# Hybrid mLSTM / RWKV-7 / S5 decoder step: the first RWKV column tile's elementwise part is issued ahead of the mLSTM gates and the S5 setup

## The chip, the cores and the metric

One core of one Trainium2 chip runs the whole step. Its engines work side by side, each through its own queue in order: TensorE (PE, with its weight loads as PEld), VectorE (DVE), ScalarE (ACT), GpSimd (POOL), and SyncE (SP), which issues most DMAs. The metric is the device time of one execution in microseconds, the median of the runs shown.

## What is computed

One layer (DEPTH is 1) over 512 prompt rows and 8 sample rows, 520 rows in all, of 1024 columns. A wide projection of the input is cut into the inputs of three mixers, whose outputs are merged and normalised:

```python
def _layer(x, st, p):
    ...
    xm, ig, fg, og, zm, rcols, zr, u, zs, gm = _split_cols(x @ p['w_in'])
    ...                                            # mLSTM branch: gates ig, fg, conv, q, k, v
    xr = rcols + p['r_mu'] * (prev - rcols)        # RWKV-7 branch
    r, kr, vr, wd, ad = jnp.split(xr, [...], axis=-1)
    wlog = -jax.nn.softplus(-_f32(p['r_w0'] + jnp.tanh(wd) @ p['r_w2'])) - 0.5
    decay = jnp.exp(-jnp.exp(wlog))
    a = jax.nn.sigmoid(_f32(p['r_a0'] + ad @ p['r_a2']))
    kk = heads(_f32(kr * p['r_k_k']))
    kk = kk / jnp.maximum(jnp.sqrt(jnp.sum(kk * kk, -1, keepdims=True)), 1e-12)
    ...
    yr, wkv_new = _rwkv7_recurrence(rh, heads(decay), kh, vh, kk, heads(a), _f32(wkv0))
    yr = _head_norm(yr, RWKV_GN_EPS).reshape(bsz, t, R_WIDTH) * _f32(p['r_ln_g']) + _f32(p['r_ln_b'])
    ...
    s_re, s_im = _s5_scan(uf, sre0, sim0, ...)     # S5 branch: lb_im = mag * jnp.sin(lam_im * dt), ...
    ...
    return layer_norm(ALPHA * x + merged @ p['w_out'], p['ln_g'], p['ln_b']), new_state
```

## The kernel before

Rows are kept transposed: a tile is 128 columns by 520 rows (two halves, 256 and 264). Every projection is exact to float32 by three passes: the weight is split into a high part `whi` (copied by ACT, L130) and a low part `wlo` (subtracted on POOL or DVE, L131), and each half is 24 matmuls of 0.12 us in one PSUM tile `g`, of which there are three. So a projected tile is 48 matmuls, about 5.7 us of PE. Whoever empties `g` lets PE go on: ACT for a mixer's own column (`rc` L350, `xr` L351), DVE for tiles projected ahead to fill PE (`us` L278 to L282, `zf` L298). `rcol` projects one RWKV column and may take a queued fill tile first.

The order of the program is: entry LayerNorm (to about 40 us), RWKV (to about 750 us), S5, mLSTM, and the final merge. In `rwkv()` the low-rank inputs come first (`rcol(24)`, Tanh), then the first part of `s5_setup` (it ends with two Sin activations, L834 and L835), then the mLSTM `gates`, then the rest of the S5 setup. Only then come the eight column tiles, in four pairs. For a tile `ct`:

- `decay(ct)`: Exp on both halves of both low-rank products (`ew`, `ta`, L460), Ln (L463), Exp (L464), a cumulative sum `cs` on DVE (L466), and four Exp of it (`pd` L471, `pc` L473, `ip` L476, and of the sample rows `smp` L477).
- `elementwise(ct)`: squares, `ss` by matmul, Relu (L492), then Ln (L494) and Exp (L495) give the reciprocal norm `inv`; DVE makes `kkn` (L497), `ar`, `bk`, `bv`. It calls `decay(ct + 1)` near its end. Last it multiplies `bk` by `pc` and transposes it to `bkt` (L570, L572).
- per pair: `inverse`, a chain of 31 steps of two DVE instructions each (`itmp` L589, `xi` L591), begun by the transpose `lu` (L579); `chain`, matmuls over the chunks with small copies between; `headnorm`, with Ln on two halves (L681) and one Exp (L682) on ACT for each tile.

A scheduler lays out the queues: the order of writing is the priority, and by its own clock it puts an instruction where its operands seem ready. So `decay`, `elementwise` and `headnorm` of the next and the last tiles are strewn through `inverse` and `chain`, and code written elsewhere moves instructions on all engines. At run time each queue goes in that order.

ACT holds one set of function tables at a time; a change of set is an instruction of its own, `ACT_TABLE_LOAD`, which the compiler puts ahead of an activation whose function the loaded set lacks. One of them is written by hand: `A.preload_act_table_set("natural_log_exp_and_others")`, L434, held behind the Tanh and the Sin by `issue_after`.

Of the kernel before, what the change touches and what calls it, by code (L numbers as in the profile page):

```python
# [8 lines left out]
F32 = mybir.dt.float32  # L9
# [6 lines left out]
P = 128  # L16
# [7 lines left out]
RH, RD, CH = 16, 64, 64  # L24
NCH = T // CH
# [14 lines left out]
def hybrid_step(ctx: ExitStack, tc: tile.TileContext, I, O):  # L40
# [317 lines left out]

    env = dict(locals())
    rwkv(tc, I, O, env)  # L360
    flc.close()
    mrg = Merge(tc, I, O, env)
# [29 lines left out]
def rwkv(tc, I, O, env):  # L392
# [3 lines left out]
    dma, pa, pc, mm, tr, pcol, inproj, gemm = e.dma, e.pa, e.pc, e.mm, e.tr, e.pcol, e.inproj, e.gemm  # L396
# [16 lines left out]
    ctx2 = ExitStack()  # L413
    rp = ctx2.enter_context(tc.tile_pool(name="rp", bufs=1, reuse_waits="tile"))
# [3 lines left out]
    def rt(name, tag="t", bufs=TB):  # L418
        return rp.tile([P, N], F32, tag=tag, bufs=bufs, name=name)
# [8 lines left out]
    xwa = rcol(24)  # L428
    th = A.activation(lora[0:64, :], xwa[0:64, :], AF.Tanh)
    V.tensor_copy(lora[64:128, :], xwa[64:128, :])  # L430
    setup = s5_setup(tc, I, O, env)
    sin = next(setup)
    with tc.issue_after(th.ins), tc.issue_after(sin.ins):
        A.preload_act_table_set("natural_log_exp_and_others")  # L434
    gates(tc, I, O, env)
    next(setup, None)
    rq = ctx2.enter_context(tc.tile_pool(name="rq", bufs=1, reuse_waits="tile"))

    def halves(f):
        for s, n in HALVES:  # L440
            f(s, n)
# [8 lines left out]
    def decay(ct):  # L450
        for j, nm in enumerate(("r_w2", "r_a2")):
            dma(w2a2[hs(j), j], I[nm][0, :, ct * P:(ct + 1) * P])

        ew, ta = rt("ew"), rt("ta")

        def lo1(s, n):
            for j, (t, b) in enumerate(((ew, e.nw0), (ta, e.na0))):
                p = pa("lw")
                mm(p[:, 0:n], w2a2[:, j], lora[:, s:s + n])
                A.activation(t[:, s:s + n], p[:, 0:n], AF.Exp, bias=b[:, ct:ct + 1], scale=-1.0)  # L460
        halves(lo1)
        for t in (ew, ta):
            A.activation(t, t, AF.Ln, bias=epst[:, 4:5])  # L463
            A.activation(t, t, AF.Exp, scale=-1.0)  # L464
        cs = rt("cs")
        V.tensor_tensor_scan(cs[:, 0:T], cstep.rearrange("p a b -> p (a b)"), ew[:, 0:T], 0.0,  # L466
                             op0=ALU.mult, op1=ALU.add)
        pd = rp.tile([P, NCH, CH + 1], F32, tag="pd", bufs=1, name="pd")
        G.memset(pd[:, :, 0:1], 1.0)
        cs3 = f3(cs)  # L470
        A.activation(pd[:, :, 1:CH + 1], cs3, AF.Exp, scale=-EH)  # L471
        pcs = rp.tile([P, NCH], F32, tag="pc", bufs=4, name="pc")
        A.activation(pcs, cs3[:, :, CH - 1], AF.Exp, scale=-EH)  # L473
        ip = rt("ip")
        ip3 = f3(ip)
        A.activation(ip3, cs3, AF.Exp, scale=EH)  # L476
        A.activation(smp[:, ct, 0, :], ew[:, T:N], AF.Exp, scale=-EH)  # L477
        return ta, pd, ip3, pcs

    def elementwise(ct, st):  # L480
        ci = ct % 2
# [16 lines left out]
        ar = rp.tile([P, 2, NCH, 2 * CH], F32, tag="ar", bufs=4, name="ar")  # L498
# [3 lines left out]
        bk = rp.tile([P, NCH, 3 * CH], F32, tag="bk", bufs=1, name="bk")  # L502
# [21 lines left out]
        bv = rt("bv", "bv", 3)  # L524
# [8 lines left out]
        yv = st["yv"]  # L533
# [8 lines left out]
        la, lr = st["la"], st["lr"]  # L542
# [17 lines left out]
                                pattern=[[0, 4], [1, 2], [1, 64]], channel_multiplier=-1)  # L560
        if ct < KT - 1:
            decays.append(decay(ct + 1))
        G.tensor_tensor(bk, bk, st["pc"][ci].unsqueeze(2).to_broadcast([P, NCH, 3 * CH]), op=ALU.mult)
        bkt = rq.tile([P, 2, NCH, CH], F32, tag="bkt", bufs=4, name="bkt")
        pvs = [pa("bt").rearrange("p (a b) -> p a b", a=NCH) for _ in range(2)]
# [103 lines left out]
    def headnorm(ct, y, bv, w):  # L669

        rng = ((0, 256), (256, 256)) if w == T else ((0, w),)
        q = rq.tile([P, T], F32, tag="yq", bufs=1, name="yq")
        for s, n in rng:
            p = pc("hm")
            mm(p[:, 0:n], e.cen, y[:, s:s + n])
            A.activation(y[:, s:s + n], p[:, 0:n], AF.Copy)
            A.activation(q[:, s:s + n], p[:, 0:n], AF.Square)
        for s, n in rng:
            p = pc("hv")
            mm(p[:, 0:n], e.bones, q[:, s:s + n])  # L680
            A.activation(q[:, s:s + n], p[:, 0:n], AF.Ln, scale=1.0 / RD, bias=epst[:, 2:3])  # L681
        A.activation(q[:, 0:w], q[:, 0:w], AF.Exp, scale=-0.5)  # L682
        V.scalar_tensor_tensor(y, y, pcol("r_ln_g", ct), q[:, 0:w], op0=ALU.mult, op1=ALU.mult)
        V.tensor_tensor(bv[:, 0:w], y, bv[:, 0:w], op=ALU.add)

    decays = [decay(0)]
    for s_ in range(4):
        st = {"ar": [0, 0], "bkt": [0, 0], "bv": [0, 0]}
        st["pc"] = [0, 0]
        st["yv"] = rp.tile([P, 2, 2, NCH, RD], F32, tag="yv", bufs=2, name="yv")  # L690
        st["la"] = rp.tile([P, 2 * NCH, CH], F32, tag="la", bufs=1, name="la")
        st["lr"] = rp.tile([P, 2 * NCH, CH], F32, tag="lr", bufs=2, name="lr")
        for ci in range(2):
            elementwise(2 * s_ + ci, st)
        inverse(st)
        yr = chain((2 * s_, 2 * s_ + 1), st)
        for ci in range(2):
            ct = 2 * s_ + ci
            bv = st["bv"][ci]
            headnorm(ct, yr[:, ci, :], bv, T)  # L700
            dma(e.ybsave[ct, :, 0:T], bv[:, 0:T])
# [19 lines left out]
    for c4 in range(2):  # L721
        p = pa("s48")
        for j in range(4):
            ct = 4 * c4 + j
# [978 lines left out]
```

## Time and profile before

| | |
|---|---|
| time, median of 3 runs | 1435.56 us (1435.4 to 1437.0) |
| the profiled execution's own time | 1430.04 us |
| its span, first to last instruction | 1428.2 us |
| mean granted TensorE clock | 0.954 |
| PE busy | 1291.1 us, 90% |
| DVE busy | 952.2 us, 67% |
| ACT busy | 618.3 us, 43% |
| POOL busy | 568.4 us, 40% |

The span is 1.8 us shorter than the same execution's time: what lies outside the first and the last instruction. In the rows further below, a stretch of a window is read by its length and each engine's busy time in it: an engine busy for the whole stretch is its limit. A timeline row gives the start, the length, and in brackets the idle time before an instruction and what ended it.

### The profile page before, as it was taken

What the parts mean: (1) busy time and instruction counts of PE and PEld (TensorE: products, weight loads), DVE (VectorE), ACT (ScalarE), POOL (GpSimd) and SP (SyncE); (2) the same over time, 40 slices, a digit from 0 to 9 for tenths busy, and PEclk for the clock granted to TensorE, in tenths of its full rate; (3) what the DMA queues carried; (4) which work ended last, traced back from release to release, by engine and by line L of the source; (5) the groups of instructions that cost most, each with busy time, mean ns of one, the idle gap of its engine ahead of it and who ended that gap; (6) DMA issues with size and microseconds to landing.
All of it is one profiled execution on the core that took longest, in us unless ns stands there. A gap on an engine that the chain in (4) does not pass through costs nothing.

```text
span 1428.2 us, 27605 instructions
## 1 busy us (share of the span) xinstructions
PE 1291.1 (90%) x10509; PEld 1162.1 (81%) x10509; DVE 952.2 (67%) x1950; ACT 618.3 (43%) x1322; POOL 568.4 (40%) x723
## 2 busy tenths in 40 slices
PE   5889989998999899998996888897899999999897
PEld 4888888877987788997976788787888798799765
DVE  6784693469336843789535997577775784665857
ACT  4446537354735463241232332232765775443230
POOL 3445544444444454447406775872000012103710
PEclk9999999999998999998998899997899999999999
DMA  5342222212221222344427453434767676466241
GB/s 181 84 117 81 80 74 63 75 42 68 66 71 42 79 64 75 96 129 149 122 69 131 105 104 91 102 77 117 225 198 255 212 224 207 149 197 194 82 118 60
DMA packets 244275, 166.92 MB, mean 117 GB/s; under 512 B 54424, under 2 KB 219674, under 8 KB 243870
## 3 DMA queue, kind: packets, MB, share of 16 engines
q1 hardware_dynamic: 244142, 165.15, 41.3%
q8 instruction: 83, 1.36, 0.4%
q14 instruction: 50, 0.41, 0.1%
HBM read 124.13 MB, written 38.68 MB: 114 GB/s over the span
## 4 chain that ended last, share of the span: by engine, by line
PE 52%; DVE 22%; POOL 8%; DMA 8%; issue 6%; ACT 3%; SPq 1%; DVEq 0%; ACTq 0%; POOLq 0%
PE g L62 33%; PE cy L62 3%; DVE xi L591 3%; DVE itmp L589 3%; PE cr L62 2%; PE gg L62 2%; POOL ph L954 1%; DVE wlo L131 1%; POOL pht L952 1%; POOL pht L953 1%; PE qk L62 1%; PE nd L62 1%; POOL et L981 1%; PE s L62 1%; PE lw L62 1%
## 5 line engine op out<-in xcount | busy, mean ns | idle before, releaser
L62 PE MATMUL g<-xh,whi 128*128 128x264 f32 (+1 forms) x1552 | 463.3, 299 | 40.2 <-DVE th L1500 15.0
L62 PE MATMUL g<-xl,whi 128*128 128x264 f32 (+1 forms) x1552 | 458.0, 295 | 1.0 <-POOL xl L217 0.5
L62 PE MATMUL g<-xh,wlo 128*128 128x264 f32 (+1 forms) x1552 | 457.2, 295 | 0.0
L62 PEld LDWEIGHTS g<-xh,whi 128*128 128x128 f32 x1552 | 303.6, 196 | 52.3 <-DVE th L1500 16.4
L62 PEld LDWEIGHTS g<-xl,whi 128*128 128x128 f32 x1552 | 303.9, 196 | 6.2 <-POOL xl L217 0.8
L62 PEld LDWEIGHTS g<-xh,wlo 128*128 128x128 f32 x1552 | 303.5, 196 | 4.9 <-issue 0.8
L130 ACT ACTIVATE whi<-wraw 128x512 fp32r<-128x512 f32 x258 | 151.6, 625 | 222.0 <-PE g L62 152.1
L131 POOL TENSOR_TENSOR wlo<-wraw,whi 128x512 fp32r<-128x512 f32 x138 | 192.7, 1416 | 134.7 <-ACT whi L130 122.6
L131 DVE TENSOR_TENSOR wlo<-wraw,whi 128x512 fp32r<-128x512 f32 x120 | 111.6, 956 | 29.5 <-ACT whi L130 27.4
L591 DVE TENSOR_TENSOR xi<-xi,itmp 128x31 f32<-128x31 f32 (+15 forms) x124 | 56.6, 456 | 3.2
L589 DVE TENSOR_TENSOR itmp<-lu,xi 128x31 f32<-128x31 f32 (+15 forms) x124 | 53.9, 435 | 3.0
L555 DVE TENSOR_TENSOR lr<-gg,maskg 64x256 f32<-64x256 f32 x32 | 13.5, 422 | 59.9 <-ACT la L554 59.8
L650 DVE SCALAR_TENSOR_TENSOR xv<-xv,pc,cy 64x64 f32<-64x64 f32 x112 | 31.2, 279 | 29.5 <-PE cy L62 24.9
L637 POOL COPY xv<-yv 64x128 f32<-64x128 f32 x64 | 24.8, 389 | 58.6 <-PE cy L62 48.2
L1547 POOL TENSOR_TENSOR mg<-mg,gth 128x256 f32<-128x256 f32 (+1 forms) x24 | 18.4, 782 | 72.6 <-DVE gth L1546 59.5
L62 PE MATMUL g<-ysh,whi 128*128 128x256 f32 (+1 forms) x128 | 38.3, 311 | 7.9 <-ACT ysh L258 5.6
L62 PE MATMUL g<-w_bmh,wlo 128*128 128x264 f32 (+1 forms) x128 | 37.5, 294 | 7.5 <-DVE wlo L131 7.4
L1547 POOL TENSOR_TENSOR mg<-mg,gt 128x256 f32<-128x256 f32 (+1 forms) x16 | 16.1, 1011 | 67.3 <-DVE gt L1546 67.3
L298 DVE COPY zf<-g 128x256 f32<-128x256 f32 (+1 forms) x56 | 23.8, 424 | 28.7 <-PE g L62 28.3
L644 DVE COPY yv<-cr 64x128 f32<-64x128 f32 x32 | 9.0, 281 | 50.2 <-PE cr L62 43.8
L1279 POOL COPY cvo<-xm 128x11 f32<-128x11 f32 x8 | 4.6, 572 | 91.9 <-ACT xm L1277 70.8
L645 ACT COPY yv<-cr 64x128 f32<-64x128 f32 x32 | 8.4, 262 | 75.6 <-DVE yv L644 75.4
(574 smaller groups left out, 3257.2 us busy)
## 6 DMA issues: line engine op xcount, KB each, us to landing
wraw<-in_w_in_dram SPq DMA_DIRECT2D x194, 256.0 KB
zsave<-zf SPq DMA_DIRECT2D x36, 260.0 KB
cn<-in_state_mlstm_c_dram SPq DMA_DIRECT2D x32, 256.0 KB
out_dram<-cn SPq DMA_DIRECT2D x32, 256.0 KB
yb<-yssave SPq DMA_DIRECT2D x16, 260.0 KB
zz<-zsave SPq DMA_DIRECT2D x16, 260.0 KB
wraw<-in_w_br_dram SPq DMA_DIRECT2D x16, 256.0 KB
wraw<-in_s_glu_w_dram SPq DMA_DIRECT2D x16, 256.0 KB
```

The costliest lines, as they stand in the source:

```text
L62: TE.matmul(out, lhsT, rhs, start=start, stop=stop)
L130: A.activation(hi[:, k, 0:m], raw[:, :, 0:m], AF.Copy)
L131: eng.tensor_tensor(lo[:, k, 0:m], raw[:, :, 0:m], hi[:, k, 0:m].bitcast(F32), op=ALU.subtract)
L298: V.tensor_copy(z[:, s:s + n], p)
L589: V.tensor_tensor(tv, lu[:, s + 1:32, s:s + 1].to_broadcast([P, r, w]), xi[:, s:s + 1, 0:w].to_broadcast([P, r, w]), op=ALU.mult)
L591: V.tensor_tensor(xi[:, s + 1:32, 0:w], xi[:, s + 1:32, 0:w], tv, op=ALU.add)
L637: G.tensor_copy(xv[hs(1 - pi), pi], yv[hs(1 - pi), pi, :, n, :])
L650: V.scalar_tensor_tensor(dst, xv[hs(pi), pi, ci, :], pcs[ci][hs(pi), n:n + 1], psn[hs(pi), ci, :], op0=ALU.mult, op1=ALU.add)
L952: G.tensor_tensor(tg[0], b(0), ph[:, q, :, 0:n], op=ALU.mult)
L953: G.tensor_tensor(tg[1], b(1), ph[:, 1 - q, :, 0:n], op=ALU.mult)
L954: G.tensor_tensor(ph[:, q, :, n:2 * n], tg[0], tg[1], op=ALU.add if q else ALU.subtract)
L1547: G.tensor_tensor(dst, dst, g, op=ALU.add)
```

## The change

`elementwise(0)` (with `decay(0)` and `decay(1)`) is written right after the Tanh and the table preload, ahead of `s5_setup` and `gates`. Its last part, the product with `pc` and the transposed rows `bkt`, becomes a function `beta_rows`, called for tile 0 behind the setup and for the others right behind their `elementwise`, as before. The preload loses its hold on the Sin, which is now written behind it.

```diff
     th = A.activation(lora[0:64, :], xwa[0:64, :], AF.Tanh)
     V.tensor_copy(lora[64:128, :], xwa[64:128, :])
-    setup = s5_setup(tc, I, O, env)
-    sin = next(setup)
-    with tc.issue_after(th.ins), tc.issue_after(sin.ins):
+    with tc.issue_after(th.ins):
         A.preload_act_table_set("natural_log_exp_and_others")
-    gates(tc, I, O, env)
-    next(setup, None)
-    rq = ctx2.enter_context(tc.tile_pool(name="rq", bufs=1, reuse_waits="tile"))
...
         if ct < KT - 1:
             decays.append(decay(ct + 1))
+        return ar, bk, bv
+
+    def beta_rows(ct, st, made):
+        ci = ct % 2
+        ar, bk, bv = made
         G.tensor_tensor(bk, bk, st["pc"][ci].unsqueeze(2).to_broadcast([P, NCH, 3 * CH]), op=ALU.mult)
...
     decays = [decay(0)]
+    st = state()
+    made = elementwise(0, st)
+
+    setup = s5_setup(tc, I, O, env)
+    next(setup)
+    gates(tc, I, O, env)
+    next(setup, None)
+    rq = ctx2.enter_context(tc.tile_pool(name="rq", bufs=1, reuse_waits="tile"))
     for s_ in range(4):
-        st = {"ar": [0, 0], "bkt": [0, 0], "bv": [0, 0]}
...
+        if s_:
+            st = state()
         for ci in range(2):
-            elementwise(2 * s_ + ci, st)
+            ct = 2 * s_ + ci
+            beta_rows(ct, st, elementwise(ct, st) if ct else made)
         inverse(st)
```

Line numbers in the pieces of order below are those of the kernel they come from: Sin is L834 in the one, L846 in the other; the Exp, Ln and Exp of `decay` are L460, L463, L464 in the one and L455, L458, L459 in the other; Ln and Exp of `inv` L494, L495 and L489, L490.

ACT's queue around the Tanh (`lora`) and the two Sin (`s`, `c`), before (`gv` are the gates' inputs):

```order
L429 ACTIVATE lora<-xr 64x520
L1131 ACTIVATE gv<-g,gbias 4x256
L834 ACT_TABLE_LOAD
L834 ACTIVATE s<-rr 128x64
L835 ACTIVATE c<-ab,epst 128x64
L434 ACT_TABLE_LOAD
L1131 ACTIVATE gv<-g,gbias 4x264
```

and with the change, first at the Tanh:

```order
L130 ACTIVATE whi<-wraw 128x512
L429 ACTIVATE lora<-xr 64x520
L432 ACT_TABLE_LOAD
L455 ACTIVATE ew<-lw,nw_319 128x256
L455 ACTIVATE ta<-lw,na_321 128x256
```

and some 70 rows on, at the Sin:

```order
L350 ACTIVATE rc<-g 128x264
L351 ACTIVATE xr<-g,omu 128x264
L846 ACT_TABLE_LOAD
L846 ACTIVATE s<-rr 128x64
L847 ACTIVATE c<-ab,epst 128x64
L480 ACTIVATE sq<-xr,par 128x520
```

The preload stood behind the Sin; it now stands ahead of it, with tile 0's Exp and Ln between, and what follows the Sin starts from the set that the Sin's load brought.

ACT's queue in the first `inverse`, where `decay(2)` lies; before:

```order
L460 ACTIVATE ew<-lw,nw_319 128x264
L463 ACTIVATE ew<-ew,epst 128x520
L460 ACTIVATE ta<-lw,na_321 128x264
L464 ACTIVATE ew<-ew 128x520
L130 ACTIVATE whi<-wraw 128x512 x2
L350 ACTIVATE rc<-g 128x264
L463 ACTIVATE ta<-ta,epst 128x520
L572 ACTIVATE bkt<-bt 128x512
L477 ACTIVATE smp<-ew 128x8
```

and with the change:

```order
L455 ACTIVATE ew<-lw,nw_319 128x264
L458 ACT_TABLE_LOAD
L458 ACTIVATE ew<-ew,epst 128x520
L455 ACT_TABLE_LOAD
L455 ACTIVATE ta<-lw,na_321 128x264
L459 ACTIVATE ew<-ew 128x520
L130 ACTIVATE whi<-wraw 128x512 x2
L350 ACTIVATE rc<-g 128x264
L458 ACT_TABLE_LOAD
L458 ACTIVATE ta<-ta,epst 128x520
L572 ACTIVATE bkt<-bt 128x512
L472 ACT_TABLE_LOAD
```

The activations are the same; a load now stands wherever a Ln follows an Exp or an Exp a Ln. It is so at every such place behind the Sin up to the end of the RWKV stage, in `inv` and in `headnorm` too. In all, ACT's queue has 18 loads before and 71 with the change: 54 new ones, less the one at L1499 (the first Tanh of the S5 merge), which is gone. By stage they stand so:

| stage | new loads |
|---|---|
| tile 1's `inv`, ahead of the first `inverse` | 2 |
| first `inverse`: `decay(2)` 4, `inv` 2 | 6 |
| first `chain`: `decay(3)` 2, `inv` 2 | 4 |
| second and third `inverse`: `decay` and `inv` 4, `headnorm` 6, each | 20 |
| second and third `chain`: `decay` 4, `inv` 2, each | 12 |
| fourth `inverse`: `headnorm` of the third pair | 4 |
| fourth `chain` and the end: sample rows 2, last `headnorm` 4 | 6 |

DVE's queue where the last rows of the S5 setup (`pks`, `ph`, `s_`) meet a tile's `kkn`; before, tile 0's:

```order
L892 COPY pks<-c_775 64x32 x2
L875 TENSOR_TENSOR pks<-pw_746,pw_747 128x256
L875 TENSOR_TENSOR s_776<-ph 128x64
L892 COPY pks<-s_776 64x32 x2
L278 COPY us<-g 128x32x8
L497 SCALAR_TENSOR_TENSOR kkn<-xr,par,inv 128x520
```

and with the change, tile 1's:

```order
L887 TENSOR_TENSOR pks<-pw_1321,pw_1322 128x256
L887 TENSOR_TENSOR s_1351<-ph 128x64
L278 COPY us<-g 128x32x8
L904 COPY pks<-s_1351 64x32 x2
L278 COPY us<-g 128x32x8
L281 COPY us<-g 128x8
L282 COPY us<-g 128x8
L492 SCALAR_TENSOR_TENSOR kkn<-xr,par,inv 128x520
```

Gates and setup stood ahead of tile 0's `kkn`; they now stand between tile 0's `bv` and tile 1's `kkn`, and six first copies `us` (L278) lie among them where five did.

## Rows read from the trace of the kernel before

**Rows 1.** The page's busy times: busy us, share of the span, instructions.
```profile
PE 1291.1 (90%) x10509; PEld 1162.1 (81%) x10509; DVE 952.2 (67%) x1950; ACT 618.3 (43%) x1322; POOL 568.4 (40%) x723
```

**Rows 2.** Stretches of the span: length, busy us (instructions) of each engine, granted clock, DMA.
```profile
60.00:80.00 20.00, 13.26 (x78) 11.96 (x77) 15.49 (x64) 5.72 (x12) 5.05 (x6) 0.74 0.42 88
...
163.00:215.00 52.00, 45.24 (x336) 43.10 (x335) 48.51 (x90) 22.78 (x48) 23.11 (x27) 0.93 0.24 66
...
300.00:356.00 56.00, 46.52 (x348) 40.55 (x344) 52.06 (x108) 26.60 (x61) 23.17 (x34) 0.94 0.20 56
356.00:440.00 84.00, 84.00 (x851) 75.18 (x849) 32.09 (x71) 43.73 (x103) 38.00 (x52) 1.00 0.25 68
```

**Rows 3.** ACT's table loads by line: count, busy us, mean ns of one, idle before.
```profile
L1258 ACT ACT_TABLE_LOAD x5 | 6.4, 1283 | 0.1
...
L434 ACT ACT_TABLE_LOAD x1 | 1.3, 1283 | 0.0
```

**Rows 4.** ACT's timeline at a load of the mLSTM stage: start us, us, instruction, [idle before].
```profile
826.38 1.28 ACT L1072 ACT_TABLE_LOAD   x1
828.73 0.41 ACT L1072 ACTIVATE yo<-ys 128x288 f32<-128x288 f32 x1 [1.07 <-PE ys L62]
```

**Rows 5.** ACT's timeline in the first `inverse`.
```profile
167.26 0.73 ACT L463 ACTIVATE ew<-ew,epst 128x520 f32<-128x520 f32 x1
...
170.11 0.72 ACT L463 ACTIVATE ta<-ta,epst 128x520 f32<-128x520 f32 x1
...
172.93 0.85 ACT L351 ACTIVATE xr<-g,omu 128x256 f32<-128x256 f32 x2
...
177.93 0.73 ACT L485 ACTIVATE sq<-xr,par 128x520 f32<-128x520 f32 x1 [3.62 <-DVE xr L356]
...
185.31 0.64 ACT L495 ACTIVATE inv<-inv 128x520 f32<-128x520 f32 x1
```

**Rows 6.** PE's waits in the first `inverse`, 163 to 215 us: us in total, times, longest.
```profile
PE g L62 <- ACT xr L351: 3.0, 1, 3.0
PE g L62 <- DVE zf L298: 2.8, 1, 2.8
```

**Rows 7.** DVE's timeline there.
```profile
180.32 0.43 DVE L298 COPY zf<-g 128x264 f32<-128x264 f32 x1 [1.73 <-PE g L62]
...
187.07 0.75 DVE L497 SCALAR_TENSOR_TENSOR kkn<-xr,par,inv 128x520 f32<-128x520 f32 x1
```

**Rows 8.** ACT's timeline in the second `inverse`.
```profile
316.29 0.83 ACT L351 ACTIVATE xr<-g,omu 128x256 f32<-128x256 f32 x2
...
330.32 0.64 ACT L495 ACTIVATE inv<-inv 128x520 f32<-128x520 f32 x1
```

**Rows 9.** DVE's timeline there.
```profile
318.41 0.74 DVE L355 SCALAR_TENSOR_TENSOR xr<-rc,par,xr 128x512 f32<-128x512 f32 x1
...
331.68 0.75 DVE L497 SCALAR_TENSOR_TENSOR kkn<-xr,par,inv 128x520 f32<-128x520 f32 x1
```

**Rows 10.** ACT's timeline in the second `chain`.
```profile
375.08 0.83 ACT L351 ACTIVATE xr<-g,omu 128x256 f32<-128x256 f32 x2
```

**Rows 11.** PE's timeline there, at the first matmul of the next half.
```profile
377.59 0.28 PE L62 MATMUL g<-xh,whi 128*128 128x264 f32 x1
```

**Rows 12.** The chain of waits from 740 to 756 us, in order of time.
```profile
743.55 2.04 PE hv L62 x4
...
745.62 0.48 ACT yq L681
...
748.75 0.92 ACT yq L681 x2
```

**Rows 13.** PE's waits from 40 to 163 us.
```profile
PE g L62 <- DVE us L278: 7.3, 4, 3.2
```

**Rows 14.** DVE's timeline around tile 1's `kkn` and the first `inverse`.
```profile
133.38 0.76 DVE L497 SCALAR_TENSOR_TENSOR kkn<-xr,par,inv 128x520 f32<-128x520 f32 x1 [4.90 <-ACT inv L495]
...
162.70 2.02 DVE L579 STREAM_TRANSPOSE lu<-la 128x1024 f32<-128x1024 f32 x1
```

More of the change, by code (lines that the diff above doesn't have):

```diff
@@ L684, in headnorm, with state @@
         V.tensor_tensor(bv[:, 0:w], y, bv[:, 0:w], op=ALU.add)
-    decays = [decay(0)]
-    for s_ in range(4):
-        st = {"ar": [0, 0], "bkt": [0, 0], "bv": [0, 0]}
[L689 to L692, printed above, removed]
+    def state():
+        return {"ar": [0, 0], "bkt": [0, 0], "bv": [0, 0], "pc": [0, 0],
+                "yv": rp.tile([P, 2, 2, NCH, RD], F32, tag="yv", bufs=2, name="yv"),
+                "la": rp.tile([P, 2 * NCH, CH], F32, tag="la", bufs=1, name="la"),
+                "lr": rp.tile([P, 2 * NCH, CH], F32, tag="lr", bufs=2, name="lr")}
+    decays = [decay(0)]
+    st = state()
[5 more added lines that the diff above has]
+    rq = ctx2.enter_context(tc.tile_pool(name="rq", bufs=1, reuse_waits="tile"))
+    for s_ in range(4):
+        if s_:
+            st = state()
         for ci in range(2):
-            elementwise(2 * s_ + ci, st)
+            ct = 2 * s_ + ci
+            beta_rows(ct, st, elementwise(ct, st) if ct else made)
         inverse(st)
```

## The prediction

> **What bounds the kernel now.** I read the busy times first. PE is busy 90% of the span, DVE 67%, ACT 43% [rows 1]: by the average nothing on ACT should matter. The stretches say more. In a `chain` stage (356 to 440 us) PE is busy for all 84 us: it is the limit, and what holds PE up there is lost outright. In an `inverse` stage (163 to 215, 300 to 356 us) DVE is busy 48.5 of 52 and 52.1 of 56 us, PE 45.2 and 46.5: the limit is DVE's chain of 31 steps, with `kkn`, `cs`, `xr` and `zf` of the neighbouring tiles strewn into the same queue. ACT is busy half of each [rows 2]. So the question is whether ACT has slack at the few places where DVE or PE wait for it, and it has little: in the first `inverse` PE waits 3.0 us for ACT's `xr` and 2.8 us for DVE's `zf` [rows 6]. The start (60 to 80 us) is the loosest place: PE 13.26 of 20 us, clock 0.74 [rows 2]; and from 40 to 163 us PE waits 7.3 us for `us` on DVE [rows 13].
>
> **What the change does at the start.** Its visible part swaps two blocks of DVE and ACT work: tile 0's elementwise part goes first, gates and setup second. Nothing is removed. Tile 0's part is then early, but the first `inverse` (162.70 us) needs tile 1's too [rows 14], and tile 1's `kkn` now stands behind gates and setup on DVE. That `kkn` waited 4.90 us for ACT, in a stretch where DVE had time [rows 14]; this room takes up part of the block. In the new order six first copies `us` stand among the block's rows where five did, so PE's waits for `us` move on rather than vanish. From both sides: at best PE's 7.3 us of waits go and the lost clock of 60 to 80 us comes back, (1 − 0.74) × 13.26 = 3.4 us, together a gain of 10.7; at worst PE waits for `us` and DVE for `inv` once more, a loss of about 7.3 + 2 loads = 10 us. Taken: 0, in the middle, since the same work still precedes the same transpose `lu`. SP's and POOL's queues get the same instructions in another order; POOL (40%) isn't waited for at any place quoted here, and I put its part at 0, within these bounds. The later `beta_rows(0)` feeds only `chain`, over 50 us on: 0, covered by the first `inverse`.
>
> **What it does to ACT: 53 table loads more.** Before, the preload of the set that holds both Ln and Exp comes behind the Sin, and the trace has no load between it and the S5 merge. With the change the Sin's load comes later, and behind it the queue has a load at each change between Ln and Exp: 54 new ones, one gone. A load takes 1283 ns in every row [rows 3], so ACT gets 53 × 1.283 = 68.0 us more work; ACT would be busy 686 us, still under half of the span. A load doesn't wait for the operands of the activation behind it: the one at 826.38 ran while `yo` was waiting for PE until 828.73 [rows 4]. It costs nothing where ACT is idle anyway, and 1.28 us where its neighbours stand back to back. What is exposed, stage by stage:
>
> - First `inverse`, 6 loads. Four (ahead of Ln at 167.26, of `ta`, of Ln at 170.11, of `smp`) stand ahead of `xr` at 172.93, in a stretch where ACT has no idle time [rows 5]: `xr` comes 4 × 1.283 = 5.1 us later. PE waits for this very `xr` already [rows 6], and DVE's `zf` for PE's next half, 1.73 us at 180.32 [rows 7]: all 5.1 pass on to DVE, the limit here. Two more stand ahead of Ln and Exp of `inv`; Exp ends at 185.95 [rows 5], `kkn` starts at 187.07 [rows 7], so 1.1 of 2.6 us is slack. **5.1 + 1.5 = 6.6.** Bounds 4 and 7.7.
> - Second and third `inverse`, 10 loads each. Four of `decay` stand ahead of `xr`, which ends at 317.12 [rows 8], while DVE takes it at 318.41 [rows 9]: 5.1 − 1.3 = 3.8. `inv` ends at 330.96 [rows 8], `kkn` starts at 331.68 [rows 9]: slack 0.7. Its two loads give 2.6 − 0.7 = 1.9 if none of ACT's idle time takes them. The six of `headnorm` stand in the same queue, but ACT has about half its time free; I let them hide. 3.8 + 1.9 = 5.7 each, **11.4** for the two (the third stage is taken to be like the second). Bounds: 3.0 each if idle time takes a part of each group, 10 × 1.283 − 2.0 = 10.8 each if nothing hides.
> - Chains, 4, 6 and 6 loads. Second `chain`: four loads stand ahead of `xr`, which ends at 375.91 [rows 10]; the next half of a projection, which needs the PSUM tile that `xr` empties, starts at 377.59 [rows 11]: 1.7 us of slack, so 5.1 − 1.7 = 3.4. The third the same. The first has two such loads: 2.6 − 1.7 = 0.9. The loads of `inv` hide, since nobody needs `inv` at once. **7.7.** Bounds 2 (scheduler's other order of the halves) and 15 × 1.28 = 19.
> - Fourth `inverse` and `chain`, 6 loads: PE has queued tiles to fill in. **1.5**, bounds 0 and 5.1.
> - The end: the last two `headnorm` stand on the chain that ends the stage, Ln at 745.62 and 748.75 right behind `hv` of PE [rows 12]; ACT waits for `hv` there under a load's length, so the four loads there (two of Ln, two of Exp) hide about 1.3 of 5.1 us. **3.8**, bounds 2.6 and 5.1.
> - Tile 1's `inv`, 2 loads: counted in the start.
>
> Sum: 6.6 + 11.4 + 7.7 + 1.5 + 3.8 = 31 us, start 0. The profiled execution took 1430.04 us and would take 1461; its median is 5.5 us higher, and the same 31 us on 1435.56 give **1467 us**. Shares of the 68 us: some 45% exposed.
>
> The rows show no idle time ahead of a load, 0.0 and 0.1 us in the mean [rows 3]. The Trainium skill ("ScalarE: Activation LUTs", section "What ACT_TABLE_LOAD costs") gives a load 1283 ns and adds a drain of some 1.38 us, 2.66 us per switch; by it ACT would get 53 × 2.66 = 141 us instead of 68, and 31 us of loss would be 64. The rows agree with the first figure and don't show the second.
>
> **Rivals.**
>
> 1. Not slower. ACT is 57% idle and a load runs ahead of its activation's wait [rows 1, 4]: if the loads fall into idle time before `xr` and `inv`, and the start gains its 10.7 us, the time is 1435.56 − 10.7 + a few = about 1428. For it: ACT's average, and the 3.62 us of idle time behind the group in the first `inverse` [rows 5]. Against it: that idle time comes after `xr`, not ahead of it. It decides at `xr`: were it needed 5.1 us or more after its end, the loads would be free; I read slacks of 0, 1.3 and 1.7 us.
> 2. All on the path. If the idle time on ACT is only the echo of DVE and PE waiting, each load counts: 1435.56 + 68 = 1504 us. For it: a loop between DVE (`zf`, `xr`), PE (`g`) and ACT in which each waits for the other. Against it: the six loads of each `headnorm` have nobody waiting closely.
> 3. A load costs more than its own row, because the activation behind it starts late. From the start of the load at 826.38 to that of `yo` at 828.73 are 2.35 us [rows 4]; were all of it the load's price, the loss would be 31 × 2.35 / 1.283 = 57 us, 1492 in all. Against it: `yo` was released by PE [rows 4]. The Trainium skill's switch with its drain (the section named above) is this case at a higher price, 1500 us.
> 4. The change doesn't do this: the set that the Sin's successor brings holds Ln and Exp both, and one load serves the stage. Then only the start counts, 1425 to 1446, middle 1435. For it: the stage before ran so, with no load behind L434. Against it: the queue of the changed kernel, which names 71 loads; that of before names 18, and the trace has 18. The Trainium skill has this rule ("ScalarE: Activation LUTs", section "Table sets: the hidden batching unit"): Ln then Exp is one load, since one set holds both. The stage of before agrees with it, by its preload; the changed queue does not.
>
> **How the numbers follow.** My forecast, 31 us with each term inside its bounds, has 0.82; rival 1 0.05, rival 2 0.07, rival 3 0.03, rival 4 0.03. Lower end of the range: 4 + 6 + 2 + 0 + 2.6 = 15, with a start 2 to 3 us better: 1448. Upper end: not all bounds at once; DVE's stages at 7.7 + 2 × 8, chains 12, the fourth pair 5, end 5, start +10 give 56: 1492. That holds the forecast's 0.82 but for its edges. A measurement of this kernel can tell about 0.2%, 2.9 us. Faster by more: rival 1 and a third of rival 4, and a start far better than taken, 0.05 in all. Within 0.2%: 0.03. Slower: the forecast, rivals 2 and 3, 0.92.
>
> **What would show it.** ACT's loads by line: 71 in all, 1283 ns each, at the lines of Ln and Exp of `decay`, `inv` and `headnorm`. ACT busy about 686 us; PE and DVE busy as before, with more idle time. The stretch from the transpose `lu` of one pair to the next should be longer by 10 us or so for each of the first three pairs; PE's waits for ACT's `xr` in the first `inverse` should grow from 3.0 to about 8 us; PE should now have waits in the chains, where it had none; the end from the last `hm` to the last `bv` should be 3.8 us longer, and `lu` of the first pair should start near 162.7 us. Wrong would make it: loads that stand in ACT's idle time at `xr`, a start that gains or loses over 10 us, or PE's clock falling in the longer waits (it is 0.93 and 0.94 in the `inverse` stages [rows 2]), which I have put into no term.

## The result and the profile after

The change makes the kernel slower: 1469.54 us (1467.58 to 1471.19) against 1435.48, a ratio of 1.0243 with an interval of 1.0218 to 1.0267, so +34 us where some +31 was forecast (1467). The profiled execution took 1468.55 us, its span is 1466.8 us.

The page of the changed kernel, busy times (answering to [rows 1]), and its loads by line, the first five groups of the Ln and Exp lines (count, busy us, mean ns, idle before; [rows 3]):

```profile
PE 1313.0 (90%) x10509; PEld 1180.6 (80%) x10509; DVE 950.8 (65%) x1950; ACT 684.0 (47%) x1375; POOL 569.9 (39%) x723
```
```profile
L458 ACT ACT_TABLE_LOAD x11 | 14.1, 1283 | 0.2
L681 ACT ACT_TABLE_LOAD x9 | 11.5, 1283 | 0.4 <-PE hv L62 0.2
L682 ACT ACT_TABLE_LOAD x8 | 10.3, 1283 | 0.1
L490 ACT ACT_TABLE_LOAD x7 | 9.0, 1283 | 0.1
L489 ACT ACT_TABLE_LOAD x6 | 7.7, 1283 | 0.1
```

ACT has 1375 instructions instead of 1322, 53 more, all of them loads, and is busy 65.7 us longer (68.0 forecast). It is still busy only 47% of the span. DVE's busy time is the same to 1.4 us. PE's is 21.9 us longer with the same 10509 matmuls: they ran at a lower mean clock, 0.935 after 0.954. Part of this is the one execution that was profiled: a second profile of the kernel before has PE busy for 1305.1 us at 0.943, and over all runs here the kernel before lies between 0.939 and 0.957, the changed one between 0.930 and 0.935. A lower clock was in no term of the sum.

ACT's timeline in the first `inverse` (answers to [rows 5]) shows what a load costs:

```profile
169.30 1.28 ACT L458 ACT_TABLE_LOAD   x1
170.60 0.73 ACT L458 ACTIVATE ew<-ew,epst 128x520 f32<-128x520 f32 x1
171.35 1.28 ACT L455 ACT_TABLE_LOAD   x1
172.64 0.48 ACT L455 ACTIVATE ta<-lw,na 128x264 f32<-128x264 f32 x1
...
174.99 1.28 ACT L458 ACT_TABLE_LOAD   x1
176.28 0.73 ACT L458 ACTIVATE ta<-ta,epst 128x520 f32<-128x520 f32 x1
176.92 0.58 ACT L572 ACTIVATE bkt<-bt 128x512 f32<-128x512 f32 x1
177.50 1.28 ACT L472 ACT_TABLE_LOAD   x1
...
180.53 0.83 ACT L351 ACTIVATE xr<-g,omu 128x256 f32<-128x256 f32 x2
```

Four loads stand ahead of `xr`, as read from the order. The Ln at 170.60 starts 1.30 us after the load before it began, the Exp at 172.64 1.29 us after its own: nothing further stands between a load and its activation. The load does end an overlap. Before, the same `ta` started 0.64 us after its Ln (167.26 [rows 5]), which had not ended:

```profile
167.90 0.46 ACT L460 ACTIVATE ta<-lw,na 128x264 f32<-128x264 f32 x1
```

Now it starts 2.04 us after it, 1.40 later. `xr` starts 15.8 us behind `lu` (164.75), before 10.2 [rows 5, 14]: 5.6 us later, where four loads make 5.1 and the lost overlaps the rest.

### The profile page after: what moved, and what is told of

It is laid out like the page before. It is cut to its first block, busy times and chain, and to the rows that moved or that the text cites. A ratio compares the mean times of both kernels' runs of the same rounds, so it can differ in the third digit from the quotient of the medians.

```text
span 1466.8 us, 27645 instructions
## 1 busy us (share of the span) xinstructions
PE 1313.0 (90%) x10509; PEld 1180.6 (80%) x10509; DVE 950.8 (65%) x1950; ACT 684.0 (47%) x1375; POOL 569.9 (39%) x723
## 5 line engine op out<-in xcount | busy, mean ns | idle before, releaser
L62 PE MATMUL g<-xh,whi 128*128 128x256 f32 (+1 forms) x1552 | 468.8, 302 | 48.3 <-DVE th L1512 17.1
L62 PE MATMUL g<-xl,whi 128*128 128x256 f32 (+1 forms) x1552 | 465.3, 300 | 0.3 <-DVE xl L217 0.3
L62 PE MATMUL g<-xh,wlo 128*128 128x256 f32 (+1 forms) x1552 | 463.4, 299 | 0.0
L62 PEld LDWEIGHTS g<-xh,whi 128*128 128x128 f32 x1552 | 311.1, 201 | 60.5 <-DVE th L1512 18.7
L62 PEld LDWEIGHTS g<-xl,whi 128*128 128x128 f32 x1552 | 310.5, 200 | 5.6 <-DVE xl L217 0.6
L62 PEld LDWEIGHTS g<-xh,wlo 128*128 128x128 f32 x1552 | 310.3, 200 | 5.1 <-issue 1.1
L131 POOL TENSOR_TENSOR wlo<-wraw,whi 128x512 fp32r<-128x512 f32 x138 | 196.1, 1438 | 161.5 <-ACT whi L130 149.0
L650 DVE SCALAR_TENSOR_TENSOR xv<-xv,pc,cy 64x64 f32<-64x64 f32 x112 | 31.2, 279 | 36.6 <-PE cy L62 33.8
L355 DVE SCALAR_TENSOR_TENSOR xr<-rc,par,xr 128x512 f32<-128x512 f32 x25 | 23.9, 958 | 27.6 <-ACT xr L351 27.5
L62 PE MATMUL g<-ysl,whi 128*128 128x256 f32 (+1 forms) x128 | 39.6, 311 | 0.0
L62 PE MATMUL g<-w_brh,wlo 128*128 128x264 f32 (+1 forms) x128 | 38.3, 301 | 1.3 <-DVE wlo L131 1.3
```

The costliest lines, as they stand in the source:

```text
L62: TE.matmul(out, lhsT, rhs, start=start, stop=stop)
L131: eng.tensor_tensor(lo[:, k, 0:m], raw[:, :, 0:m], hi[:, k, 0:m].bitcast(F32), op=ALU.subtract)
L355: V.scalar_tensor_tensor(x[:, 0:T], rc[:, 0:T], mu, x[:, 0:T], op0=ALU.mult, op1=ALU.add)
L650: V.scalar_tensor_tensor(dst, xv[hs(pi), pi, ci, :], pcs[ci][hs(pi), n:n + 1], psn[hs(pi), ci, :], op0=ALU.mult, op1=ALU.add)
```

## The experiments

The times of before beside them were 1434.82 us (first four) and 1435.13 (next four).

**The load put back.** One line more in the changed kernel:

```diff
     setup = s5_setup(tc, I, O, env)
-    next(setup)
+    with tc.issue_after(next(setup).ins): A.preload_act_table_set("natural_log_exp_and_others")
     gates(tc, I, O, env)
```

> The change, with one more preload of the Ln and Exp set behind the Sin. Order on every engine as in the changed kernel, 19 table loads instead of 71. Theory (the whole loss is the added loads): 1430 to 1440 us, the same as before within some 3 us. Rival (the move of tile 0's part costs by itself, at the start or by the order it gives the later stages): 1445 us or more.

1429.84 us, ratio to before 0.9963 (0.9940 to 0.9985). The whole loss, 1469.54 − 1429.84 = 39.7 us, is the loads', and the move by itself is a gain of some 5 us, 0.4%. This kernel is faster than both.

**The loads without the move.** The kernel before, its preload written ahead of the setup:

```diff
-    setup = s5_setup(tc, I, O, env)
-    sin = next(setup)
-    with tc.issue_after(th.ins), tc.issue_after(sin.ins):
+    with tc.issue_after(th.ins):
         A.preload_act_table_set("natural_log_exp_and_others")
+    setup = s5_setup(tc, I, O, env)
+    sin = next(setup)
```

> The kernel before, unmoved, only its preload stands ahead of the Sin. Order on every engine as before, 84 table loads instead of 18 (13 more than in the changed kernel, at the gates and at tile 0, since here the Sin comes earlier). Theory (the loads alone cost it): 34 us as in the changed kernel and 0 to 8 us for the 13 loads at the start, 1468 to 1478 us. Rival (the move costs a good part): under 1460 us.

1487.65 us, 1.0379 (1.0348 to 1.0410): +52.8 us for 66 loads. The loads alone cost time in the kernel before too, but this is some 10 us above the range expected: the start was priced wrongly. The first `lu` starts at 177.72 us instead of 162.70: the 15 loads ahead of it (19.2 us) cost 15.0 us, where 0 to 8 were expected. PE's waits from 40 to 178 us (total, times, longest) show the route; before, `us` had 7.3 [rows 13] and ACT's `xr` 1.9:

```profile
PE g L62 <- ACT xr L351: 12.0, 3, 6.5
PE g L62 <- DVE us L278: 9.9, 4, 5.4
```

**The move without its side effect.** The first part of the S5 setup, with its Sin, and the hold of the preload go back ahead of tile 0:

```diff
+    setup = s5_setup(tc, I, O, env)
+    sin = next(setup)
-    with tc.issue_after(th.ins):
+    with tc.issue_after(th.ins), tc.issue_after(sin.ins):
         A.preload_act_table_set("natural_log_exp_and_others")
...
-    setup = s5_setup(tc, I, O, env)
-    next(setup)
     gates(tc, I, O, env)
```

> The move without its side effect: the first part of the S5 setup with the Sin and the hold of the preload stay where they were, only tile 0's elementwise part goes ahead of the gates and the rest of the setup. 18 table loads. Theory: 1430 to 1440 us. Rival (the move costs by itself): 1445 us or more. If the start's idle time on PE could be recovered by the move (rival 1's second half), 1425 to 1430 us.

1429.66 us, 0.9971 (0.9955 to 0.9988): the same as with the load put back.

**Which loads.** In three kernels one group's Ln (and Exp) became Relu with the same operands, so that its loads vanish while every queue keeps its order; a fourth does all three. The edit of `decay`; those of `inv` (L489, L490) and `headnorm` (L681, L682) are alike:

```diff
-            A.activation(t, t, AF.Ln, bias=epst[:, 4:5])
+            A.activation(t, t, AF.Relu, bias=epst[:, 4:5])
```

> The changed kernel with Relu in place of the two Ln of each decay (same bias, same shape), which leaves the logarithm out of the decays: 49 loads instead of 71, order unchanged. By the terms of the prediction the decay loads carry 5.1 + 7.6 + 7.7 = 20 us: 1449 us. Rival, every load costs the same share (34 / 53 = 0.64 us): 22 x 0.64 = 14 us, 1455 us. Rival, the decay loads hide and those of inv and headnorm carry the loss: 1463 us or more.

> The changed kernel with Relu in place of Ln and Exp of headnorm (same bias and scale, same shapes), which leaves the reciprocal root of the head norm out: 55 loads instead of 71, order unchanged. By the prediction's terms these 16 loads carry the end's 3.8 us and some 1 us else: 1464 to 1465 us. Rival, by count (34 / 53 = 0.64 us each): 10 us, 1459 us. Rival, the six that stand together in each inverse stage don't hide: 15 us or more, under 1455 us.

> The changed kernel with Relu in place of Ln and Exp of inv, which leaves the reciprocal norm of kk out: 58 loads instead of 71, order unchanged. By the prediction's terms 1.5 + 2 x 1.9 = 5.3 us: 1464 us. By count 8.3 us: 1461 us. Without decay's 22 loads the kernel took 26 us less, and without all some 40 us less; if the groups add up, those of headnorm and inv have 14 us between them.

> All three groups with Relu, as the three kernels apart: 20 loads, order unchanged; the logarithm of decay and the Ln and Exp of inv and headnorm are left out. A control of the method: if only the loads matter and Relu costs what Ln and Exp cost, the time is that of the kernel with the load behind the Sin, 1430 us, within 4 us. If the functions themselves matter, it is under 1425 us.

| left out of the changed kernel | loads | time, us | less than 1469.54 by | by load |
|---|---|---|---|---|
| `decay`'s | 22 | 1443.46 | 26.1 | 1.19 |
| `headnorm`'s | 16 | 1463.63 | 5.9 | 0.37 |
| `inv`'s | 13 | 1464.59 | 5.0 | 0.38 |
| all three | 51 | 1430.33 | 39.2 | 0.77 |

In the total the groups add up: 26.1 + 5.9 + 5.0 = 37.0 of 39.2. All three together give the time of the kernel with the load put back, so Relu for Ln and Exp is no effect of its own. A load of `decay` costs 93% of its 1.283 us, one of the others 30%. `inv` and `headnorm` came out as the terms had them (5.3 and some 5 us), `decay` larger (20.4). With four runs of each kernel these differences are good to 3 or 4 us: that clears `decay` of both its rivals, but the 8.3 us that `inv` would have by count is not excluded.

**Only the early loads.** One more preload behind the second `inverse`:

```diff
-            A.activation(t1[a:a + 32, 0], t1[a:a + 32, 1], AF.Copy)
+            cp = A.activation(t1[a:a + 32, 0], t1[a:a + 32, 1], AF.Copy)
+        if st["last"]:
+            with tc.issue_after(cp.ins): A.preload_act_table_set("natural_log_exp_and_others")
...
+        st["last"] = s_ == 1
         inverse(st)
```

> The changed kernel with one more preload behind the second inverse (its copy out of the transposed inverse): the loads up to there stay (22), those behind it are gone, 41 in all, order unchanged. Theory (each stage's loads cost what that stage grew by, independent of later stages): by the traces of the changed kernel and of the one with the load behind the Sin, the second inverse ends 14.3 us later (367.7 against 353.4), so 1429.8 + 14 = 1444 us. Rival (the lost time is given back later, or the loss comes from the later stages alone): under 1437 us. Rival (early loss makes later stages slower too): over 1450 us.

1446.74 us, 1.0076 (1.0043 to 1.0108), 2.7 us above the theory's number. Its stages up to there are as long as with all loads (54.9, 86.7, 61.8 us), the later ones as short as without (87.6, 55.3, 82.8). A loss is neither given back nor passed on, and both rivals fall. In this one profile the first `lu` started at 167.67 us, 2.9 us behind the changed kernel's; but the profiled execution took 1444.82 us, so that doesn't explain what the median is over.

**Where the 5 us of the move come from.** Both kernels once more, for second profiles:

> The kernel before once more, for a second profile of it. The kernel with the load behind the Sin is some 5 us faster by the times, but its RWKV stage ends no earlier (754.5 against 751.1 us); what lies behind that stage took 668.8 us against 677.1. If the gain lies in the later order, the part behind the RWKV stage is again about 677 us here. If it was a chance of one profile, it is anywhere from 668 to 678 us.

> The kernel with the load behind the Sin once more, for a second profile of it. If the gain lies in the later order, the part behind the RWKV stage takes 667 to 674 us here; if it was a chance of one profile, it may be 677 us as before.

Behind the RWKV stage the kernel before took 680.3 us (677.1 in the first profile), the other 672.1 (668.8). The stage itself ended at 755.8 and 751.1 us before, at 752.4 and 754.5 with the move. So by these profiles the gain lies in the later part, not at the start. Seven other kernels with the move spread from 671.6 to 677.1 us there; all nine profiles with the move have a mean of 673.3 us, the two without 678.7. Which of the instructions that the move reorders there brings it was not tried; the cause stays open.

## Why the prediction was right, and where it was not

Each stage from the first `lu` to the next (DVE's `lu` L579 and, between them, `lu` L597, the transpose that ends the 31 steps), by the traces; without the loads: the mean of the two profiles of the kernel with the load put back, which has the changed kernel's order on every engine.

| stage | without loads, us | changed kernel | difference | forecast |
|---|---|---|---|---|
| up to the first `lu` | 163.2 | 164.75 | +1.6 | 0 |
| first `inverse` | 49.9 | 54.72 | +4.8 | 6.6 |
| first `chain` | 87.9 | 86.51 | −1.3 | 0.9 |
| second `inverse` | 52.4 | 61.71 | +9.3 | 5.7 |
| second `chain` | 87.1 | 93.95 | +6.8 | 3.4 |
| third `inverse` | 56.1 | 62.91 | +6.8 | 5.7 |
| third `chain` | 83.9 | 90.72 | +6.9 | 3.4 |
| fourth pair and the end | 173.0 | 177.38 | +4.3 | 5.3 |
| behind it | 670.5 | 674.15 | +3.7 | 0 |

The sum of the differences is 42.9 us, the difference of the spans; by the medians it is 39.7. A single stage is less sure than the sum: without the loads the two profiles differ by up to 3.7 us in a stage (third `chain`, 82.0 and 85.7). Pair by pair, `inverse` and `chain` together grew by 3.5, 16.1 and 13.7 us, where about 10 each was expected. The number came out within 3 us by luck, because two errors met: the loads cost 8.7 us more than the 31 of the sum, and the move, put at 0, gains 5.

1. **The mechanism** was right: 71 loads of 1283 ns, and of the 66.7 us of the 52 loads that the first experiment takes away 39.7 came through. Rival 1 falls by the time, and rival 4 by the 71 loads that ran. Rival 2, each load on the path, is nearly right for `decay` alone. Rival 3 falls by the rows above: 1.30 us from the start of a load to its activation. By the Trainium skill's 2.66 us per switch ("ScalarE: Activation LUTs", section "What ACT_TABLE_LOAD costs") ACT would have got 141 us more; it got 65.7, and the trace shows the 1283 ns, the lost overlap of some 0.1 us and no drain. The Trainium skill's rule that Ln then Exp is one load (same page, section "Table sets: the hidden batching unit") holds where the joint set was loaded by hand, as the first experiment shows with 19 loads, and fails in the changed kernel, where each change has a load.

2. **The chains were mis-sized**: 12.4 us where 7.7 were forecast, 13.7 in the second and third against 6.8. In the second the step that failed is the route. I let `xr` hold up PE by a PSUM tile with 1.7 us of slack. What came late was an earlier instruction: DVE's `cs` (L461), which waits for `decay`'s `ew`, and behind it in DVE's queue stands `xv` (L650), the recurrence of `chain`. DVE's timeline in the second `chain`, first of the changed kernel, then with the load put back (start, length, idle before):

```profile
384.47 0.28 DVE L644 COPY yv<-cr 64x128 f32<-64x128 f32 x1 [2.94 <-PE cr L62]
389.98 1.22 DVE L461 TENSOR_TENSOR_SCAN cs<-cstep,ew 128x512 f32<-128x512 f32 x1 [5.22 <-ACT ew L459]
391.12 1.19 DVE L650 SCALAR_TENSOR_TENSOR xv<-xv,pc,cy 64x64 f32<-64x64 f32 x4
```
```profile
370.17 0.28 DVE L644 COPY yv<-cr 64x128 f32<-64x128 f32 x1 [2.94 <-PE cr L62]
372.98 1.23 DVE L461 TENSOR_TENSOR_SCAN cs<-cstep,ew 128x512 f32<-128x512 f32 x1 [2.52 <-ACT ew L459]
374.12 1.19 DVE L650 SCALAR_TENSOR_TENSOR xv<-xv,pc,cy 64x64 f32<-64x64 f32 x4
```

`cs` waits 5.22 us instead of 2.52, two loads more, and with it `xv`, by which PE's next step is held. PE's row in the changed kernel:

```profile
391.42 0.95 PE L62 MATMUL cr<-xv,ar 128*64 128x64 f32 x6 [2.14 <-DVE xv L650]
```

Without the loads PE has no such wait in this stage. Then PE's clock. Windows of 5 us of the changed kernel (length, PE busy, clock, DMA), then of the kernel with the load put back, then of the second profile of the kernel before:

```profile
380.00:385.00 5.00, 5.00 (x30) 0.75 0.01 3
385.00:390.00 5.00, 4.28 (x43) 1.00 0.44 118
390.00:395.00 5.00, 3.58 (x27) 0.77 0.00 0
395.00:400.00 5.00, 5.00 (x27) 0.55 0.00 0
400.00:405.00 5.00, 5.00 (x43) 1.00 0.51 143
```
```profile
363.00:368.00 5.00, 5.00 (x45) 0.68 0.00 0
...
373.00:378.00 5.00, 5.00 (x60) 1.00 0.39 106
378.00:383.00 5.00, 5.00 (x42) 1.00 0.16 59
383.00:388.00 5.00, 5.00 (x47) 1.00 0.41 103
```
```profile
361.00:366.00 5.00, 5.00 (x25) 0.50 0.44 108
```

Behind the 2.14 us of waiting the granted clock is 0.77 and 0.55 for 10 us, 27 matmuls of `g` and others in a window where 42 to 60 go at 1.00. But it fell without a wait too, while PE was busy throughout: to 0.75 in the changed kernel shortly ahead of the wait, to 0.68 with the load put back, to 0.50 in the kernel before, whose whole stage there took 90.16 us at 0.94, all of it busy. What this one wait did to the clock is therefore not shown. Over the whole stage, changed kernel, then without `decay`'s loads:

```profile
367.69:461.64 93.95, 91.50 (x864) 81.27 (x863) 32.48 (x74) 53.50 (x110) 39.70 (x53) 0.94 0.22 59
```
```profile
357.38:444.64 87.26, 86.92 (x867) 77.21 (x866) 32.68 (x74) 48.09 (x107) 40.07 (x53) 1.00 0.23 64
```

In this pair PE idles 2.45 us instead of 0.34 and is busy 4.6 us longer on the same work at 0.94 of the clock. Over all profiles of kernels with the move, the three with `decay`'s loads in this stage took 91.8 to 94.0 us (PE busy 89.4 to 91.5), the six without 86.6 to 88.1 (busy 86.4 to 87.9). By the means the loads cost 5.3 us here, 2.4 of idle PE and 3.0 of slower matmuls; the clock's part was in no term.

In the third `chain` the route of the forecast did come. PE waits for ACT's `xr`, 4.2 us where 3.4 were forecast, and idles 5.5 us of this stage, without the loads 0.05:

```profile
554.90 0.59 PE L62 MATMUL g<-xh,whi 128*128 128x264 f32 x1 [4.17 <-ACT xr L351]
```

3. **The `inverse` stages** were right in sum, 20.9 us against 18.0, not each. In the first I took PE's wait of 3.0 us for `xr` [rows 6] for one on the `xr` behind the four loads. It is a later one, which itself waits for POOL; ACT's and PE's timelines of the kernel before:

```profile
192.22 0.85 ACT L351 ACTIVATE xr<-g,omu 128x256 f32<-128x256 f32 x2 [3.99 <-POOL shn L353]
```
```profile
192.75 0.39 PE L62 MATMUL g<-xh,whi 128*128 128x264 f32 x1 [3.02 <-ACT xr L351]
```

The first `xr` ends at 173.78 [rows 5] and DVE takes it at 176.61: 2.8 us of slack where I had read none. In the changed kernel DVE waits for ACT like this:

```profile
173.68 1.23 DVE L461 TENSOR_TENSOR_SCAN cs<-cstep,ew 128x512 f32<-128x512 f32 x1 [1.86 <-ACT ew L459]
...
181.46 0.75 DVE L355 SCALAR_TENSOR_TENSOR xr<-rc,par,xr 128x512 f32<-128x512 f32 x1 [0.64 <-ACT xr L351]
...
193.42 0.76 DVE L492 SCALAR_TENSOR_TENSOR kkn<-xr,par,inv 128x520 f32<-128x520 f32 x1 [1.54 <-ACT inv L490]
```

That is 2.5 us by `decay`'s four loads, where 5.1 were forecast, again most of it at `cs`, and 1.5 by `inv`'s, as forecast; without `decay`'s loads the stage took 2.8 us less, without `inv`'s 1.7. In the second and third I let `headnorm`'s loads hide, and four of `decay` count 3.8 by `xr`. DVE's waits that ACT ends in the second are these:

```profile
328.88 0.75 DVE L355 SCALAR_TENSOR_TENSOR xr<-rc,par,xr 128x512 f32<-128x512 f32 x1 [0.44 <-ACT xr L351]
...
339.62 0.75 DVE L683 SCALAR_TENSOR_TENSOR yr<-yr,par,yq 128x512 f32<-128x512 f32 x1 [1.34 <-ACT yq L682]
...
345.07 0.76 DVE L492 SCALAR_TENSOR_TENSOR kkn<-xr,par,inv 128x520 f32<-128x520 f32 x1 [2.59 <-ACT inv L490]
```

`kkn` waits 2.59 us, near the 1.9 of the term; `yr` of `headnorm` stands in DVE's queue among the steps and waits 1.34, which the term had hidden; `xr`, the term's 3.8, makes DVE wait 0.44. DVE, the limit there, was busy 49.74 of 53.65 us before and 48.60 of 61.71 now: 13.1 us idle instead of 3.9. Most of that is none of these three. DVE waits 6.8 us for PE, with the load put back 0.7, and PE in its turn waits for ACT, at its transposes `bt` of `bk`:

```profile
321.76 1.11 PE L570 MATMUL bt<-ident,bk 64*128 64x64 f32 x8 [1.10 <-ACT ta L455]
326.33 1.12 PE L570 MATMUL bt<-ident,bk 64*128 64x64 f32 x8 [1.47 <-ACT bkt L572]
```
```profile
327.83 0.28 DVE L664 COPY wo<-wf 64x128 f32<-64x128 f32 x1 [1.98 <-PE wf L81]
```

PE's granted clock was 0.50 from 316 to 331 us there, and 1.00 in this stage with the load put back. These are `decay`'s loads: without them the stage took 54.44 us, 7.3 less; without `headnorm`'s 60.46 and without `inv`'s 60.05. So the term that was mis-sized is `decay`'s, 3.8 where 7.3 were lost, and the route by `xr` was wrong here too. The sum over the `inverse` stages came out near because `decay`'s term was too large in the first and too small in the second. In the third stage the groups don't add up so, one profile each: 2.3 us less without `decay`'s loads, 2.2 and 0.4 more without `headnorm`'s and `inv`'s, 6.8 less without all three.

4. **The end** was right: the loads stand back to back with what they serve. From the first `hm` (`headnorm`'s matmul for the mean) of the last tiles to the last `bv` (L684) the kernel before takes 10.0 us (741.18 to 751.14), the one with the load put back 11.8 (742.76 to 754.51) and in its second profile 10.7, the changed one 14.8 (777.85 to 792.65): 3.0 to 4.1 us by the loads, where 3.8 were forecast. With the move, `hm` has a wait of 0.75 us for ACT that the kernel before does not have there. ACT's timeline there in the changed kernel:

```profile
781.97 1.28 ACT L681 ACT_TABLE_LOAD   x1 [0.24 <-PE hv L62]
783.26 0.84 ACT L681 ACTIVATE yq<-hv,epst 128x256 f32<-128x256 f32 x2
784.12 1.28 ACT L682 ACT_TABLE_LOAD   x1
785.41 0.63 ACT L682 ACTIVATE yq<-yq 128x512 f32<-128x512 f32 x1
```

5. **The start** was right within 2 us: the first `lu` at 164.75 us, 162.7 forecast, and 163 without the loads. The idle time of PE that 60 to 80 us had [rows 2] is gone in the changed kernel (20.00 of 20 us busy there) and comes back from 100 to 165 us, so nothing is won by the swap at this place. The move's gain of 5 us, put at 0, came where I had not looked, behind the RWKV stage.

## What to carry to other kernels

When code with transcendental activations is moved, list the table loads of both compiled queues: the activations can be the same and the loads four times as many, if a function of another set comes to stand behind a hand-written preload. A load counts by the slack of the one instruction that needs its activation next, and by what stands behind that instruction in its own queue; ACT's busy share of 43% said nothing about it. Where PE is the limit, read its clock as well as its waits: in the second `chain` the loads cost as much by slower matmuls as by idle time. And read the clock from several profiles, since it falls in stages without a wait too.

## What the runs showed of the hardware

A table load puts 1.28 to 1.31 us between the activation before and the one behind it, without a further drain; where the two overlapped without it, it delays the second by some 1.4 us.

PE's clock differs from one execution of a kernel to the next, 0.934 to 0.955 in the twelve runs with the load put back, and in a `chain` it fell to 0.50 for 5 us with PE busy all the time. The loads lower it further: 0.930 to 0.935 in the four runs of the changed kernel, whose profile has PE busy for 1313.0 us on unchanged work, against 1300.5 and 1288.5 with the load put back. Behind waits of 2.1 us (second `chain`) and 4.2 us (third) stand windows of 5 us at 0.55 and 0.50; that the waits bring this about is not shown.
